# First modulation in column groups, tokens ahead of weights, and gate products one step later: a hybrid diffusion block on one core

## The chip, the cores and the metric

The kernel runs on one core of a Trainium2 chip. The metric is device time in microseconds (us), as the median of several executions. One more execution was taken with the hardware profiler; everything said of single instructions comes from it.

## What is computed

One layer of a diffusion backbone with 256 latent and 256 context tokens of width 2048, in float32.

- Two modulation vectors, one for the latent stream and one for the context: `silu(c) @ w_mod + b_mod`, 12288 wide. Its first 4096 columns are the shift and the scale of the first norm, and both streams need them; the others are needed for the latent stream alone.
- `h = rmsnorm(x) * (1 + scale) + shift` for both streams, then one projection `h @ w_in` to 7168 columns: q, two forget gates, v and an output gate for eight heads (HGRN2), and the input and the gate of a second recurrence (RG-LRU).
- HGRN2: a gated linear recurrence in both directions per head. RG-LRU: a depthwise convolution, then per block of 128 channels two gates `sigmoid(xc @ wa + ba)` and `sigmoid(xc @ wx + bx)` per direction, and a linear scan in both directions.
- The output projection, a gated residual, a second norm and modulation, a GEGLU MLP with a width-3 convolution (5632 wide), and the last gated residual.

## The kernel before, in words

All large products run in a split form: a float32 weight block is turned into a rounded high half (ACT, line 165) and the low half (DVE, line 180), tokens likewise, and three products (high-high, high-low, low-high) are added. A plain float32 product needs no split, and shows in the profile as two records.

The work is a list of **entries**, one per weight block of up to 1 MB. `run` (line 213) goes through them in order: for each chunk of an entry it emits the halves that are due (`split_to`, two halves ahead), then one step of every live generator (`step`, line 191), then the entry's products. So what a generator emits at one step stands on PE ahead of that chunk's products. A weight block lands in a ring of three buffers (`fetch`, line 140, on SP's queue); a buffer is asked for again only when its block has been used, or split where it has halves.

**First stage** (lines 287 to 411, 497 to 628). Entries 0 to 31 are the first modulation, 8 groups of 512 columns in 4 blocks each, shift and scale in turn (`add_mod1`, line 307). A block holds 4 x 128 rows of the weights by 512 columns. In blocks 0 to 15 (`whole`) the stationary operand is the 128 x 2 pair of both streams' vectors, in float32 (line 317). In blocks 16 to 31 weights are split and the stationary operand has 4 columns, high and low halves of both vectors (lines 323 and 324); the 4 x 2 table `sel` adds them up. When a group is whole, `mod1_sums` (line 335) copies it to SBUF and turns it into columns with four small products (line 343), and `mod1_scale` (line 354) makes the modulated tokens for four chunks of 128 channels: the high half on ACT (line 370), the value again on DVE or POOL (line 372), the low half on DVE (line 374). Between them stand 12 early entries (`add_early`, line 383): four groups of channels, three entries each, for the first six 128-column blocks of the projection, 24 products in each entry. Their place is the list `due` (line 404). The first entry of the list has to see every modulated chunk emitted before it (`after=("h1_gen",)`).

Tokens come in four quarters of 1 MB (`load_x`, line 500). The first is asked for after three weight blocks; the others from `first_norm` (line 596), one a step. `first_norm` squares them (ACT, line 603), adds them up (DVE, lines 605 to 609), gets sums over channels by products (`token_sums`), the inverse root, a broadcast over partitions (`spread`), and multiplies the tokens on POOL (line 623).

**Mixer stage** (lines 668 to 998). The other 50 blocks of the projection run in the order of `ORDER`. Three long chains go on beside them, a step per chunk: `mod2_all`, which accumulates the second modulation on DVE (line 689); the tree over a head's tokens (`tree`, line 866); and `rg_all`, one `rg_chain` (line 753) for each of the eight blocks of the second recurrence. A chain makes the convolved tokens, their high half `xh` (line 767) and low half `xl` (line 768) on DVE, yields, and emits the gates' six products of direction 0 (`gates(0)`, lines 776 to 778). At the end of a head the square of its output is written over `qa` (line 955), summed by two products (line 960), and copied by DVE in the same step (line 961). `qa` has one buffer, and so the next head's first write (line 872) waits for those products. `g_gen` (line 973) broadcasts a head's norm into one of the two small banks that the gates use too, and reads it on DVE (line 980).

```
    for c in range(e["nt"]):
        split_to(ahead(i, c))
        ...
        step()
        e["mm"](c, (lambda h: ring[e["half0"] + h]) if e["nh"] else fetched[i])
```

Of the kernel before, what the change touches and what calls it, by code (L numbers as in the profile page):

```python
# [17 lines left out]
KC = D // 128  # L18
T = 256
# [30 lines left out]
def dit_block_kernel(  # L50
# [55 lines left out]
    def P(name, k=0, n=1):  # L106
        o = _SM[name] + k
        return sm[:, o:o + n]

    ident = cp.tile([128, 128], F32, name="ident")  # L110
    masks = cp.tile([128, 7, 128], U8, name="masks")
    sel = cp.tile([4, 2], F32, name="sel")
    ones = cp.tile([128, 1], F32, name="ones")
    dve.memset(ones, 1.0)

# [132 lines left out]
    def tasks_after(gen):  # L248
        gens.insert(sum(g.__name__ not in BACK for g in gens), gen)
# [57 lines left out]
    def add_mod1(g, q, after, whole):  # L307

        rows = 2 if whole else 4

        def mm(c, get):
            if q == 0:
                mod1["ps"] = sbank(g // 4)
            ps = mod1["ps"][0:rows, :]
            for k in range(4):
                if whole:
                    pe.matmul(ps, cs[:, :, 4 * q + k], get[:, k * 512:(k + 1) * 512],  # L317
                              start=(q == 0 and k == 0), stop=(q == 3 and k == 3))
                    continue
                wh, wl = get(k // 2)  # L320
                cc = c4[:, 4 * q + k, :]
                s = slice(k % 2 * 512, (k % 2 + 1) * 512)
                pe.matmul(ps, cc, wh[:, s], start=(q == 0 and k == 0), stop=False)  # L323
                pe.matmul(ps, cc, wl[:, s], start=False, stop=(q == 3 and k == 3))  # L324

        def done():
            if q == 3:
                tasks_after(after(mod1["ps"], sel if rows == 4 else ident[0:2, 0:2]))
        add_entry(src=wmod[g, q], nt=1, nh=0 if whole else 2, mm=mm, done=done)


    s1 = cp.tile([128, 2, KC], F32, name="s1")
    sh1 = cp.tile([128, 2, KC], F32, name="sh1")

    def mod1_sums(ps, sel):
        n = sel.shape[0]
        sb = tp.tile([4, 512], F32, name="msb", tag="msb", bufs=2)[0:n, :]
        act.activation(sb, ps[0:n, :], AF.Copy)
        yield
        if n == 4:  # L340
            yield
        for j in range(4):
            pe.matmul(ps[:, 2 * j:2 * j + 2], sb[:, j * 128:(j + 1) * 128], sel, start=True, stop=True)
        yield
        return ps[:, 0:8].rearrange("p (j w) -> p w j", w=2)

    def mod1_shift(g):
        def gen(ps, sel):
            v = yield from mod1_sums(ps, sel)
            b = P("bm", 4 * g, 4)[:, None, :].to_broadcast([128, 2, 4])  # L350
            dve.tensor_tensor(sh1[:, :, 4 * g:4 * g + 4], v, b, op=OP.add)
        return gen

    def mod1_scale(g):
        def h1_gen(ps, sel):
            v = yield from mod1_sums(ps, sel)
            b = P("bm", 16 + 4 * g, 4)[:, None, :].to_broadcast([128, 2, 4])
            g0 = P("g", 4 * g, 4)[:, None, :].to_broadcast([128, 2, 4])
            d = s1[:, :, 4 * g:4 * g + 4]
            dve.tensor_tensor(d, v, b, op=OP.add)  # L360
            dve.scalar_tensor_tensor(d, d, 1.0, g0, op0=OP.add, op1=OP.mult)
            if g:
                yield
            while not xdone:
                yield
            for kc in range(4 * g, 4 * g + 4):
                f = tp.tile([128, 512], F32, name="hf", tag="hf", bufs=2)
                for w in range(2):
                    t = slice(w * 256, (w + 1) * 256)
                    act.activation(h1["hh"][:, kc, t], xk(kc)[:, t], AF.Identity,  # L370
                                   bias=sh1[:, w, kc:kc + 1], scale=s1[:, w, kc:kc + 1])
                    (pool if 0 < g < 3 else dve).tensor_scalar(
                        f[:, t], xk(kc)[:, t], s1[:, w, kc:kc + 1], sh1[:, w, kc:kc + 1], op0=OP.mult, op1=OP.add)
                dve.tensor_tensor(h1["hl"][:, kc, :], f, h1["hh"][:, kc, :].bitcast(F32), op=OP.subtract)
                if kc % 2:
                    yield
        return h1_gen


# [21 lines left out]
        add_entry(src=wearly[g, third], nt=2, nh=1, mm=mm, done=done, after=("h1_gen",))  # L401


    due = iter((15, 17, 19, 23, 25, 27, 29, 31, 32, 32, 32, 32))
    todo = [(g, third) for g in range(4) for third in range(3)]
    n = next(due)
    for i in range(32):
        g, q = divmod(i, 4)
        g, kind = divmod(g, 2)
        add_mod1(4 * kind + g, q, (mod1_shift, mod1_scale)[kind](g), i < 16)  # L410
        while todo and n == i + 1:
            add_early(*todo.pop(0))
            n = next(due, None)
# [80 lines left out]
            add_down(half, u)  # L494


    nc.sync.dma_start(sel, sel_d)
    fetch()

    def load_x(q):  # L500
        nc.sync.dma_start(xk(4 * q, 4), xs[:, 4 * q:4 * q + 4, :])
    load_x(0)
    nc.sync.dma_start(ident, ident_d)
    mf32 = tp.tile([128, 7 * 128], F32, name="mf32")


    cs = cp.tile([128, 2, KC], F32, name="cs")
    c4 = cp.tile([128, KC, 4], F32R, name="c4")
# [3 lines left out]
    cv = cs.rearrange("p w k -> p k w")  # L512
    c4v = c4.rearrange("p k (w s) -> p k w s", s=2)
    act.activation(c4v[:, :, :, 0], cv, AF.Copy)
    dve.tensor_tensor(c4v[:, :, :, 1], cv, c4v[:, :, :, 0].bitcast(F32), op=OP.subtract)

    lb = cp.tile([128, 2 * NH], F32, name="lb")
    oml = cp.tile([128, 2 * NH], F32, name="oml")
# [42 lines left out]
    def sqrt_table():  # L561

        act.activation(dummy, ones, AF.Sqrt)
# [30 lines left out]
    xdone = []  # L594

    def first_norm():
        qs = tp.tile([128, 2, 512], F32, name="qs0")
        for q in range(4):
            if q < 3:
                load_x(q + 1)  # L600
            for i in range(4 * q, 4 * q + 4, 2):
                sq = tp.tile([128, 2, 512], F32, name="sq", tag="sq", bufs=2)
                act.activation(sq, xk(i, 2), AF.Square)
                if i:
                    dve.tensor_tensor(qs, qs, sq, op=OP.add)
                else:
                    dve.tensor_copy(qs, sq)
# [145 lines left out]
    def rg_chain(b, x):  # L753
# [17 lines left out]
        def gates(d):  # L771
            pg = {}
            for w in (1, 0):
                pg[w] = sbank()
                c = slice((2 * d + w) * 128, (2 * d + w + 1) * 128)
                pe.matmul(pg[w], wh[:, c], xh, start=True, stop=False)
                pe.matmul(pg[w], wh[:, c], xl, start=False, stop=False)
                pe.matmul(pg[w], wl[:, c], xh, start=False, stop=True)
            return pg
        pg = gates(0)  # L780
        yield
        for d in range(2):
            k = 8 * d + b
            r, iv, th, t = (hq.tile([128, 512], F32, name=n, tag=n) for n in ("r", "iv", "th", "t"))
            for w, dst, bn in ((1, iv, "bx"), (0, r, "ba")):
                act.activation(dst, pg[w], AF.Sigmoid, bias=P(bn, k))
            yield
            act.activation(th, r, AF.Tanh, scale=sp4[:, k:k + 1])
# [77 lines left out]
    def tree(h, q):  # L866
# [477 lines left out]
```

## Time and profile before

| what | value |
|---|---|
| median of 3 executions | 1631.26 us (1630.3 to 1632.11) |
| the profiled execution | 1630.65 us |
| its span, from the first to the last instruction | 1628.9 us |
| PE, TensorE's products | busy 1566.8 us, 96% |
| DVE | busy 1207.4 us, 74% |
| ACT | busy 891.8 us, 55% |
| POOL | busy 121.0 us, 7% |
| DMA | 329.66 MB, 202 GB/s over the span |
| mean granted clock of TensorE | 0.984 of 2.4 GHz |

The span is the stretch that the profile covers; the execution's own time is 1.75 us more. PE is TensorE's products, PEld its weight loads, which lie beside products. A share of busy time is an average over stages with different limits, so a stage is read by itself. In a timeline, a bracket gives the idle time of the engine before an instruction and what ended it. A product's record is longer than its share of the engine, since products overlap in the array: the distance from start to start is its price.

### The profile page before, as it was taken

To read this page: it belongs to the slowest core of one execution; us is meant where nothing else is said; L and a number is where in the kernel's file an instruction comes from. 1 tells how busy PE (TensorE), PEld (TensorE's weight loads), DVE (VectorE), ACT (ScalarE), POOL (GpSimd) and SP (SyncE) were. 2 spreads that over 40 slices of the span, in tenths; PEclk is the share of its full clock that TensorE was granted. 3 is DMA by queue.
4 is the path that set the end of the run, shared out by engine and by line. 5 is a ranking of instruction groups with operands and counts; after the bars stand their busy time and mean duration, and the time that the engine had idled before them with its cause. 6 is when DMAs were issued, how large, how long until landed. Compare 5 with 4: busy or idle time off the path is not lost.

```text
span 1628.9 us, 25405 instructions
## 1 busy us (share of the span) xinstructions
PE 1566.8 (96%) x9904; PEld 1371.2 (84%) x9904; DVE 1207.4 (74%) x2033; ACT 891.8 (55%) x1284; POOL 121.0 (7%) x101
## 2 busy tenths in 40 slices
PE   7999899999999999899999999999999999999997
PEld 1355687778788888799999999999999999888886
DVE  2666597889888769678658788888888877656656
ACT  2355685767674456486455644444444445455553
POOL 0511000000000000000220111111111111000000
PEclk9999999999999999999999999999999999999999
DMA  8676544455455565536862466666666555655552
GB/s 355 236 283 225 193 162 149 158 172 174 167 197 199 183 206 186 183 124 238 318 224 94 171 228 230 226 231 226 229 227 227 201 181 190 221 184 197 191 200 110
DMA packets 75584, 329.66 MB, mean 202 GB/s; under 512 B 8392, under 2 KB 8520, under 8 KB 45128
## 3 DMA queue, kind: packets, MB, share of 16 engines
q1 hardware_dynamic: 75176, 327.53, 56.9%
q8 instruction: 77, 1.26, 0.3%
q10 hardware_dynamic: 288, 0.52, 0.1%
q14 instruction: 43, 0.35, 0.1%
HBM read 325.92 MB, written 2.10 MB: 201 GB/s over the span
## 4 chain that ended last, share of the span: by engine, by line
PE 79%; DVE 11%; ACT 4%; issue 3%; DMA 2%; POOL 1%; SPq 0%; DVEq 0%; ACTq 0%; POOLq 0%
PE mb L266 12%; PE mb L267 12%; PE mb L268 12%; PE mb L458 5%; PE lv L266 5%; PE lv L267 5%; PE lv L268 5%; PE lv L458 4%; PE sd L458 4%; PE sd L317 3%; DVE wl L180 2%; PE xb L458 2%; DVE macc L689 2%; PE sd L324 1%; PE sd L323 1%
## 5 line engine op out<-in xcount | busy, mean ns | idle before, releaser
L165 ACT ACTIVATE wh<-wf 128x1024 fp32r<-128x1024 f32 x424 | 445.3, 1058 | 508.4 <-PE mb L267 166.5
L180 DVE TENSOR_TENSOR wl<-wf,wh 128x1024 fp32r<-128x1024 f32 x440 | 535.7, 1223 | 155.1 <-ACT wh L165 151.2
L266 PE MATMUL mb<-hh,wh 128*128 128x512 f32 (+1 forms) x800 | 282.9, 354 | 0.0
L268 PE MATMUL mb<-hh,wl 128*128 128x512 f32 (+1 forms) x800 | 273.4, 342 | 0.0
L267 PE MATMUL mb<-hl,wh 128*128 128x512 f32 (+1 forms) x800 | 273.2, 342 | 0.0
L266 PE MATMUL mb<-h2h,wh 128*128 128x258 f32 x672 | 190.6, 284 | 0.0
L268 PE MATMUL mb<-h2h,wl 128*128 128x258 f32 x672 | 190.2, 283 | 0.0
L267 PE MATMUL mb<-h2l,wh 128*128 128x258 f32 x672 | 190.1, 283 | 0.0
L266 PE MATMUL lv<-h2h,wh 128*128 128x258 f32 x656 | 186.0, 284 | 0.0
L268 PE MATMUL lv<-h2h,wl 128*128 128x258 f32 x656 | 185.6, 283 | 0.0
L267 PE MATMUL lv<-h2l,wh 128*128 128x258 f32 x656 | 185.5, 283 | 0.0
L268 PEld LDWEIGHTS mb<-hh,wl 128*128 128x128 f32 x800 | 152.8, 191 | 17.9
L267 PEld LDWEIGHTS mb<-hl,wh 128*128 128x128 f32 x800 | 153.7, 192 | 15.9
L266 PEld LDWEIGHTS mb<-hh,wh 128*128 128x128 f32 x800 | 153.5, 192 | 15.3
L689 DVE SCALAR_TENSOR_TENSOR macc<-wm,cs,macc 128x512 f32<-128x512 f32 x180 | 136.3, 757 | 7.3 <-DMA wm<-in_wmod_dram 6.2
L267 PEld LDWEIGHTS mb<-h2l,wh 128*128 128x128 f32 x672 | 127.4, 190 | 0.0
L268 PEld LDWEIGHTS mb<-h2h,wl 128*128 128x128 f32 x672 | 126.9, 189 | 0.0
L266 PEld LDWEIGHTS mb<-h2h,wh 128*128 128x128 f32 x672 | 126.8, 189 | 0.0
L267 PEld LDWEIGHTS lv<-h2l,wh 128*128 128x128 f32 x656 | 124.4, 190 | 0.0
L268 PEld LDWEIGHTS lv<-h2h,wl 128*128 128x128 f32 x656 | 123.9, 189 | 0.0
L266 PEld LDWEIGHTS lv<-h2h,wh 128*128 128x128 f32 x656 | 123.7, 189 | 0.0
L1040 DVE TENSOR_TENSOR al<-actt,ah 128x256 fp32r<-128x256 f32 x88 | 37.8, 431 | 86.2 <-ACT ah L1039 86.2
(344 smaller groups left out, 2861.8 us busy)
## 6 DMA issues: line engine op xcount, KB each, us to landing
wf<-in_wup_dram SPq DMA_DIRECT2D x88, 1024.0 KB, 4.9
wm<-in_wmod_dram SPq DMA_DIRECT2D x256, 256.0 KB, 5.1
wf<-in_win_dram SPq DMA_DIRECT2D x50, 1024.0 KB, 4.8
wf<-in_wdn_dram SPq DMA_DIRECT2D x44, 1024.0 KB, 4.8
wf<-in_wmod_dram SPq DMA_DIRECT2D x32, 1024.0 KB, 5.7
wf<-in_wout_dram SPq DMA_DIRECT2D x16, 1024.0 KB, 5.1
wf<-in_wearly_dram SPq DMA_DIRECT2D x12, 512.0 KB, 5.5
oy<-in_xs_dram SPq DMA_DIRECT2D x2, 1024.0 KB, 13.4
```

The source lines that it names most:

```text
L165: act.activation(wh, w, AF.Copy)
L180: lo.tensor_tensor(wl, fetched[j][:, h * H:(h + 1) * H], wh.bitcast(F32), op=OP.subtract)
L266: pe.matmul(ps, wh[:, w], hh, start=(i == 0), stop=False)
L267: pe.matmul(ps, wh[:, w], hl, start=False, stop=False)
L268: pe.matmul(ps, wl[:, w], hh, start=False, stop=(i == KC - 1))
L317: pe.matmul(ps, cs[:, :, 4 * q + k], get[:, k * 512:(k + 1) * 512], start=(q == 0 and k == 0), stop=(q == 3 and k == 3))
L323: pe.matmul(ps, cc, wh[:, s], start=(q == 0 and k == 0), stop=False)
L324: pe.matmul(ps, cc, wl[:, s], start=False, stop=(q == 3 and k == 3))
L458: pe.matmul(dn["ps" + str(half)][tb * 2 + n], a[:, t], w[:, s], start=(kc == 0 and first), stop=(kc == NJ - 1 and last))
L689: dve.scalar_tensor_tensor(acc, w, cc, acc, op0=OP.mult, op1=OP.add)
L1040: dve.tensor_tensor(al, actt[:, kc, :], ah.bitcast(F32), op=OP.subtract)
```

## The change

It has four parts. (1) All 32 blocks of the first modulation take float32 products, none is split. The stationary operand is padded to 32 columns (`cpad`), and the four products of a block go to four groups of 32 columns of TensorE and to four groups of 32 partitions of one bank; the table `sel4` adds the four groups up in the small products that turn sums into columns. (2) All tokens are loaded ahead of the first weight block, the norm's sums are made in one step, and the multiplication of the tokens goes from POOL to DVE; the modulated value is made on ACT, and DVE makes its high and low halves. (3) The list `due` puts early entries further forward. (4) In `rg_chain` a yield stands ahead of `gates(0)`, and the one in the loop moves behind the tanh; a head's square goes to a buffer of the tag `qc`, and the copy of its sums comes a step later.

```diff
-    sel = cp.tile([4, 2], F32, name="sel")
...
+    cpad = tp.tile([128, KC, 32], F32, name="cpad")
+    sel4 = tp.tile([128, 2], F32, name="sel4")
+
+    def add_mod1(g, q, after):
         def mm(c, get):
             if q == 0:
                 mod1["ps"] = sbank(g // 4)
-            ps = mod1["ps"][0:rows, :]
             for k in range(4):
-                if whole:
-                    pe.matmul(ps, cs[:, :, 4 * q + k], get[:, k * 512:(k + 1) * 512],
-                              start=(q == 0 and k == 0), stop=(q == 3 and k == 3))
-                    continue
-                wh, wl = get(k // 2)
-                cc = c4[:, 4 * q + k, :]
-                s = slice(k % 2 * 512, (k % 2 + 1) * 512)
-                pe.matmul(ps, cc, wh[:, s], start=(q == 0 and k == 0), stop=False)
-                pe.matmul(ps, cc, wl[:, s], start=False, stop=(q == 3 and k == 3))
+                pe.matmul(mod1["ps"][32 * k:32 * k + 32, :], cpad[:, 4 * q + k, :], get[:, k * 512:(k + 1) * 512],
+                          start=(q == 0), stop=(q == 3), tile_position=(0, 32 * k))
...
+    def mod1_sums(ps):
+        sb = tp.tile([128, 512], F32, name="msb", tag="msb", bufs=2)
+        act.activation(sb, ps, AF.Copy)
         yield
-        if n == 4:
-            yield
         for j in range(4):
-            pe.matmul(ps[:, 2 * j:2 * j + 2], sb[:, j * 128:(j + 1) * 128], sel, start=True, stop=True)
-        yield
+            pe.matmul(ps[:, 2 * j:2 * j + 2], sb[:, j * 128:(j + 1) * 128], sel4, start=True, stop=True)
...
-            if g:
-                yield
             while not xdone:
                 yield
             for kc in range(4 * g, 4 * g + 4):
                 f = tp.tile([128, 512], F32, name="hf", tag="hf", bufs=2)
                 for w in range(2):
                     t = slice(w * 256, (w + 1) * 256)
-                    act.activation(h1["hh"][:, kc, t], xk(kc)[:, t], AF.Identity,
-                                   bias=sh1[:, w, kc:kc + 1], scale=s1[:, w, kc:kc + 1])
-                    (pool if 0 < g < 3 else dve).tensor_scalar(
-                        f[:, t], xk(kc)[:, t], s1[:, w, kc:kc + 1], sh1[:, w, kc:kc + 1], op0=OP.mult, op1=OP.add)
+                    act.activation(f[:, t], xk(kc)[:, t], AF.Identity, bias=sh1[:, w, kc:kc + 1], scale=s1[:, w, kc:kc + 1])
+                dve.tensor_copy(h1["hh"][:, kc, :], f)
                 dve.tensor_tensor(h1["hl"][:, kc, :], f, h1["hh"][:, kc, :].bitcast(F32), op=OP.subtract)
-                if kc % 2:
-                    yield
...
-    due = iter((15, 17, 19, 23, 25, 27, 29, 31, 32, 32, 32, 32))
+    due = iter((11, 13, 15, 19, 21, 23, 27, 29, 32, 32, 32, 32))
...
-    nc.sync.dma_start(sel, sel_d)
-    fetch()
-
     def load_x(q):
         nc.sync.dma_start(xk(4 * q, 4), xs[:, 4 * q:4 * q + 4, :])
-    load_x(0)
+    for q in range(4):
+        load_x(q)
     nc.sync.dma_start(ident, ident_d)
+    fetch()
...
+    dve.memset(cpad, 0.0)
+    dve.tensor_copy(cpad[:, :, 0:2], cs.rearrange("p w k -> p k w"))
+    dve.tensor_tensor(sel4, ident[:, 0:2], ident[:, 32:34], op=OP.add)
+    for j in (64, 96):
+        dve.tensor_tensor(sel4, sel4, ident[:, j:j + 2], op=OP.add)
...
     def first_norm():
+        sqrt_table()
         qs = tp.tile([128, 2, 512], F32, name="qs0")
-        for q in range(4):
-            if q < 3:
-                load_x(q + 1)
-            for i in range(4 * q, 4 * q + 4, 2):
...
-            yield
+        for i in range(0, KC, 2):
...
         sums = token_sums([qs[:, 0, :]], 4, lbank)
-        yield
         c = rq[:, :, 0:4]
         rsqrt(c[:, 0, :], sums, 1.0 / D, c[:, 1, :], c[:, 2, :])
         yield
         pb = spread(c[:, 0, :], 4, lbank)
-        yield
         rb0 = tp.tile([128, 512], F32, name="rb0")
         act.activation(rb0, pb, AF.Copy)
         for kc in range(KC):
-            pool.tensor_tensor(xk(kc), xk(kc), rb0, op=OP.mult)
+            dve.tensor_tensor(xk(kc), xk(kc), rb0, op=OP.mult)
...
+        yield
         pg = gates(0)
         yield
         for d in range(2):
...
                 act.activation(dst, pg[w], AF.Sigmoid, bias=P(bn, k))
-            yield
             act.activation(th, r, AF.Tanh, scale=sp4[:, k:k + 1])
+            yield
             act.activation(r, r, AF.Exp, scale=sp8[:, k:k + 1])
...
-        sq = qa[:, 0, :]
+        sq = hq.tile([128, T], F32, name="qc", tag="qc", bufs=3)
         act.activation(sq, po, AF.Square)
         yield
         pq = lbank()
         for b in range(2):
             pe.matmul(pq[:, b:b + 1], sq[:, b * 128:(b + 1) * 128], ones, start=True, stop=True)
+        yield
         dve.tensor_copy(ssq[:, 2 * h:2 * h + 2], pq[:, 0:2])
```

## Rows read from the trace of the kernel before

**Rows 1.** Stretches: from:to and length, busy us (instructions) by engine, PEclk, DMA, GB/s

```profile
core 0: us, PE busy (x) PEld busy (x) DVE busy (x) ACT busy (x) POOL busy (x), PEclk, DMA share, GB/s
...
0.00:8.64 8.64, 0.00 (x0) 0.03 (x1) 0.45 (x3) 1.75 (x3) 0.19 (x4) 1.00 0.80 294
8.64:20.00 11.36, 11.36 (x21) 2.00 (x22) 2.05 (x3) 3.22 (x4) 0.00 (x0) 1.00 1.01 405
...
70.00:163.00 93.00, 87.04 (x365) 51.34 (x363) 58.69 (x72) 50.81 (x61) 12.34 (x17) 0.96 0.68 249
...
189.00:760.00 571.00, 543.26 (x3173) 477.51 (x3172) 468.76 (x816) 374.05 (x563) 0.00 (x0) 0.97 0.52 175
```

**Rows 2.** Chain of waits, first 200 us: start us, us, what

```profile
49.35 13.82 PE sd L317 x32
...
187.89 0.25 PE xb L394
```

**Rows 3.** Timeline of PE, split blocks: start us, us, instruction

```profile
102.28 0.40 PE L323 MATMUL sd<-wh,c 128*4 128x512 f32 x1
...
106.92 0.40 PE L323 MATMUL sd<-wh,c 128*4 128x512 f32 x1
```

**Rows 4.** Timeline of PE, from block 31 to the end of the early projections

```profile
161.78 0.39 PE L324 MATMUL sd<-wl,c 128*4 128x512 f32 x1
162.84 1.05 PE L343 MATMUL sd<-sel,msb 4*128 4x2 f32 x8 [0.68 <-ACT msb L338]
...
171.82 0.50 PE L394 MATMUL mb<-hh,wl 128*128 128x512 f32 x1 [1.57 <-DVE wl L180]
...
173.53 0.39 PE L392 MATMUL mb<-hh,wh 128*128 128x512 f32 x1
...
187.27 0.39 PE L392 MATMUL xb<-hh,wh 128*128 128x512 f32 x1
```

**Rows 5.** Groups by line, DVE, 0 to 50 us: busy us, mean ns, idle before

```profile
L605 DVE TENSOR_TENSOR qs<-qs,sq 128x1024 f32<-128x1024 f32 x7 | 8.6, 1225 | 5.9 <-ACT sq L603 5.6
...
L607 DVE COPY qs<-sq 128x1024 f32<-128x1024 f32 x1 | 0.7, 694 | 12.6 <-ACT sq L603 12.6
```

**Rows 6.** DMA issues: KB each, median us from issue to landing

```profile
wf<-in_wup_dram SPq DMA_DIRECT2D x88, 1024.0 KB, 4.9
```

**Rows 7.** Waits of PE, from 188 us on: us in total, times, longest

```profile
PE sd L776 <- DVE xh L767: 16.7, 6, 4.5
PE sd L776 <- DVE oy L980: 4.1, 1, 4.1
...
PE sd L777 <- DVE xl L768: 0.7, 4, 0.2
```

**Rows 8.** Timeline of PE, the two longest waits of the gates' products

```profile
199.58 0.76 PE L776 MATMUL sd<-xh,gh 128*128 128x512 f32 x1 [4.46 <-DVE xh L767]
...
447.93 0.76 PE L776 MATMUL sd<-xh,gh 128*128 128x512 f32 x1 [3.95 <-DVE xh L767]
```

**Rows 9.** Stretches (columns as in rows 1) behind waits of the gates' products

```profile
199.00:205.00 6.00, 5.42 (x13) 4.06 (x14) 5.96 (x10) 4.83 (x8) 0.00 (x0) 0.52 0.79 286
...
351.00:355.00 4.00, 4.00 (x12) 3.16 (x11) 3.97 (x8) 2.19 (x4) 0.00 (x0) 0.57 0.25 66
447.50:454.00 6.50, 6.07 (x14) 4.56 (x15) 6.40 (x14) 0.72 (x2) 0.00 (x0) 0.50 0.81 295
682.00:697.00 15.00, 8.16 (x37) 6.52 (x36) 11.80 (x24) 7.72 (x14) 0.00 (x0) 0.66 0.39 132
```

**Rows 10.** A stretch of the mixer stage (columns as in rows 1)

```profile
360.00:380.00 20.00, 20.00 (x114) 17.34 (x113) 19.67 (x40) 15.34 (x27) 0.00 (x0) 1.00 0.49 172
```

**Rows 11.** Line 960 of a head's end, who waited for it: us, times

```profile
  DVE ssq L961: 16.5, 4
  DVE qa L872: 11.2, 3
```

**Rows 12.** Timeline of DVE, end of the second recurrence's block 7

```profile
740.36 0.42 DVE L810 TENSOR_TENSOR oy<-oy,r 128x256 f32<-128x256 f32 x1
...
747.00 0.42 DVE L818 TENSOR_TENSOR oy<-oy,gl 128x256 f32<-128x256 f32 x1 [1.20 <-ACT gl L816]
```

More of the change, by code (lines that the diff above doesn't have):

```diff
@@ L305, in dit_block_kernel @@
     mod1 = {}
-    def add_mod1(g, q, after, whole):
-        rows = 2 if whole else 4
+    cpad = tp.tile([128, KC, 32], F32, name="cpad")
+    sel4 = tp.tile([128, 2], F32, name="sel4")
+    def add_mod1(g, q, after):
         def mm(c, get):
@@ L313, in mm, with gen @@
                 mod1["ps"] = sbank(g // 4)
-            ps = mod1["ps"][0:rows, :]
             for k in range(4):
-                if whole:
-                    pe.matmul(ps, cs[:, :, 4 * q + k], get[:, k * 512:(k + 1) * 512],
-                              start=(q == 0 and k == 0), stop=(q == 3 and k == 3))
-                    continue
-                wh, wl = get(k // 2)
-                cc = c4[:, 4 * q + k, :]
-                s = slice(k % 2 * 512, (k % 2 + 1) * 512)
-                pe.matmul(ps, cc, wh[:, s], start=(q == 0 and k == 0), stop=False)
-                pe.matmul(ps, cc, wl[:, s], start=False, stop=(q == 3 and k == 3))
+                pe.matmul(mod1["ps"][32 * k:32 * k + 32, :], cpad[:, 4 * q + k, :], get[:, k * 512:(k + 1) * 512],
+                          start=(q == 0), stop=(q == 3), tile_position=(0, 32 * k))
         def done():
             if q == 3:
-                tasks_after(after(mod1["ps"], sel if rows == 4 else ident[0:2, 0:2]))
-        add_entry(src=wmod[g, q], nt=1, nh=0 if whole else 2, mm=mm, done=done)
+                tasks_after(after(mod1["ps"]))
+        add_entry(src=wmod[g, q], nt=1, nh=0, mm=mm, done=done)
     s1 = cp.tile([128, 2, KC], F32, name="s1")
     sh1 = cp.tile([128, 2, KC], F32, name="sh1")
[L335 to L338, printed above, removed]
+    def mod1_sums(ps):
+        sb = tp.tile([128, 512], F32, name="msb", tag="msb", bufs=2)
+        act.activation(sb, ps, AF.Copy)
         yield
-        if n == 4:
-            yield
         for j in range(4):
-            pe.matmul(ps[:, 2 * j:2 * j + 2], sb[:, j * 128:(j + 1) * 128], sel, start=True, stop=True)
-        yield
+            pe.matmul(ps[:, 2 * j:2 * j + 2], sb[:, j * 128:(j + 1) * 128], sel4, start=True, stop=True)
         return ps[:, 0:8].rearrange("p (j w) -> p w j", w=2)
     def mod1_shift(g):
-        def gen(ps, sel):
-            v = yield from mod1_sums(ps, sel)
+        def gen(ps):
+            v = yield from mod1_sums(ps)
             b = P("bm", 4 * g, 4)[:, None, :].to_broadcast([128, 2, 4])
@@ L354, in mod1_scale, with h1_gen @@
     def mod1_scale(g):
-        def h1_gen(ps, sel):
-            v = yield from mod1_sums(ps, sel)
+        def h1_gen(ps):
+            v = yield from mod1_sums(ps)
             b = P("bm", 16 + 4 * g, 4)[:, None, :].to_broadcast([128, 2, 4])
@@ L409, in dit_block_kernel @@
         g, kind = divmod(g, 2)
-        add_mod1(4 * kind + g, q, (mod1_shift, mod1_scale)[kind](g), i < 16)
+        add_mod1(4 * kind + g, q, (mod1_shift, mod1_scale)[kind](g))
         while todo and n == i + 1:
@@ L494, in dit_block_kernel @@
             add_down(half, u)
-    nc.sync.dma_start(sel, sel_d)
-    fetch()
     def load_x(q):
         nc.sync.dma_start(xk(4 * q, 4), xs[:, 4 * q:4 * q + 4, :])
-    load_x(0)
+    for q in range(4):
+        load_x(q)
     nc.sync.dma_start(ident, ident_d)
+    fetch()
     mf32 = tp.tile([128, 7 * 128], F32, name="mf32")
     cs = cp.tile([128, 2, KC], F32, name="cs")
-    c4 = cp.tile([128, KC, 4], F32R, name="c4")
     sg = tp.tile([128, 32], F32, name="csg")
@@ L511, in dit_block_kernel @@
     dve.tensor_tensor(cs.rearrange("p w k -> p (w k)"), sg, P("c", 0, 32), op=OP.mult)
[L512 to L515, printed above, removed]
+    dve.memset(cpad, 0.0)
[3 more added lines that the diff above has]
+        dve.tensor_tensor(sel4, sel4, ident[:, j:j + 2], op=OP.add)
     lb = cp.tile([128, 2 * NH], F32, name="lb")
@@ L596, in first_norm @@
     def first_norm():
+        sqrt_table()
         qs = tp.tile([128, 2, 512], F32, name="qs0")
-        for q in range(4):
-            if q < 3:
-                load_x(q + 1)
-            for i in range(4 * q, 4 * q + 4, 2):
[L602 to L607, printed above, removed]
-            yield
+        for i in range(0, KC, 2):
+            sq = tp.tile([128, 2, 512], F32, name="sq", tag="sq", bufs=2)
+            act.activation(sq, xk(i, 2), AF.Square)
+            if i:
+                dve.tensor_tensor(qs, qs, sq, op=OP.add)
+            else:
+                dve.tensor_copy(qs, sq)
         dve.tensor_tensor(qs[:, 0, :], qs[:, 0, :], qs[:, 1, :], op=OP.add)
@@ L786, in rg_chain @@
                 act.activation(dst, pg[w], AF.Sigmoid, bias=P(bn, k))
+            act.activation(th, r, AF.Tanh, scale=sp4[:, k:k + 1])
             yield
-            act.activation(th, r, AF.Tanh, scale=sp4[:, k:k + 1])
             act.activation(r, r, AF.Exp, scale=sp8[:, k:k + 1])
```

## The prediction

> **What bounds the kernel now.** I began with the table of stretches [rows 1]. TensorE is busy 95% of 189 to 760 us and 94% of 70 to 163, so it is the bound; the DMA engines run full (405 GB/s) only in the first 20 us, and PE does nothing before 8.64. So in the first stage I count the order of PE's products, and further on PE's idle time.
>
> The chain of waits then gives the price of a product of the first modulation [rows 2]: 32 records in 13.82 us, 0.432 each. A float32 product leaves two records, so one weight block (four products, 1 MB) costs 3.46. In the split form [rows 3] twenty records lie 4.64 us apart, 0.232 each; eight to a block make 1.86. An early projection is 24 products at 0.229 (60 steps in 13.74 us [rows 4]), 5.5 us. Block 31's last record ends at 161.78 + 0.39 = 162.2 [rows 4] and the last early product at 188.1 [rows 2]: a tail of 26 us. In that tail PE waits once, 1.57, for the low half of a weight that stands on DVE behind the last modulated tokens.
>
> In the mixer stage PE's waits [rows 7] name one cause above all: the gates' first product waits for xh, six times, 16.7 us, plus 0.7 for xl and once 4.1 for a bank that DVE's line 980 still reads. The two longest are in [rows 8]. Behind long ones the granted clock is low [rows 9]: 0.50 of 2.4 GHz, the lower of its two levels, behind the wait that ended at 447.93.
>
> **The change, part by part: the first stage.** Removed are the split of 16 blocks (32 conversions on ACT, 32 subtractions on DVE) and its products; all 32 blocks now take four float32 products, each on 32 columns of its own. What such products cost beside one another is nowhere in the trace. Ends: all eight records one after another, 3.46 a block, plus the time in flight that a record has after its successor's start (0.39 against a step of 0.229 [rows 4], 0.16) at four changes of column group, makes 4.1; all four groups at once, 0.86 and a little, 0.95. I take a value between, 1.9, from the order of the program: the two records of one product use the same columns and follow each other, so only the second of one product and the first of the next can run together; that is four slots of 0.432 a block, 1.73, and one half-covered slot where a run of blocks ends.
>
> Tokens first: the small parameters (0.34 MB), 4.19 MB of tokens, ident and a block make 5.65 MB ahead of the first product. By 8.64 us 294 GB/s had brought 2.54 MB; the rest at 405 takes 7.7 [rows 1]: block 0 lands at 16.3 instead of 8.6. The sum of squares now stands on DVE behind the addition that waits for ident (about 14 us), and its own additions are 8.6 + 0.7 us [rows 5] and a last one of 0.6: about 25. The token sums are placed ahead of block 2, so PE, free at 20.8, waits there to about 25.5; the sums (1.05, as the like products of [rows 4]), block 2, the norm's small steps and the broadcast (2.4, an estimate) and block 3 end near 32.7. The ring holds three blocks, so block 5 was asked for only after block 2 (28.4) and lands 4.9 later [rows 6]; from there a block comes every 2.55 us (1.05 MB at 411 GB/s, an estimate close to the 405), and block 10 ends near 49.7. The sixteen multiplications by the norm move from POOL to DVE, 0.62 each (half of 1.23 [rows 5]), 10 us, from 29 to 40: the first modulated tokens are due at 44, so they hide; without that cover they would push the first early projection one for one.
>
> From there PE has 21 blocks at 1.9 (39.9), eight early projections at 5.5 (44.0) and five sums of 1.05 (5.3): 89. Each early projection also waits for its halves, since the ring gives its buffer back only after the subtraction: about 1 us each, 8. Block 31 ends at 147. In the tail DVE makes two passes a chunk instead of three; I take 0.7 off: 25.3, so 172 against 188.1. **Minus 16 us**; 0.95 a block would give minus 32, 4.1 plus 39.
>
> A rule of the Trainium skill speaks against it: TensorEngine Tiling (Array Packing), Key Properties, says that changing the tiling mode drains TensorE. No row shows such a change; as an estimate, some 32 changes between 32 and 128 columns at the 0.16 in flight would make the sum 1599 instead of 1594.
>
> **The gates.** With a further step between xl and the gates' products PE has one more chunk of twelve products (2.74 us) to do before them. Of the six waits only two are longer: 4.46 leaves 1.7 and 3.95 leaves 1.2 [rows 8]; the other 8.3 and the 0.7 go. The 4.1 for the bank [rows 7] leaves 1.4 at most, as the broadcast then belongs to an earlier step. Removed: 5.5 + 9.0 + 2.7 = 17.2. Clock: (1 - clock) times the stretch, idle time left out, is 2.9, 1.7, 3.2 and 3.0 in the four of [rows 9], about 10 in all. Together 27. I give 7 back: DVE is nearly full where this happens (19.67 of 20 us [rows 10]), and PE's idle time is when it catches up, so some of it returns as waits for weights' low halves. Tanh one yield earlier changes no work.
>
> The head's square goes into a free buffer, and its sums' copy one step later: DVE now waits 16.5 and 11.2 us for these products [rows 11]. DVE is not the bound, so I count nothing for it but the 20 kept above. The gates' chain gets a step longer: block 7's ends at 740.4 and its gated product comes at 747.0 [rows 12], 6.6 of slack for 2.74. **Minus 20 us**, between minus 28 (all kept) and plus 3 (all comes back, and one step more at the end).
>
> **Sum.** The profiled execution took 1630.65 (span 1628.9 and 1.75 around it), 0.6 under the median shown: 1630.65 - 16 - 20 = 1594.6, say 1594. A measurement here tells about 0.2%, 3.3 us, from no change.
>
> **Rivals.**
> A. All four column groups at once, 0.95 a block. For: in the sum above the groups share no columns. Against: the second record of a product stands in program order ahead of the next group's first. DMA then sets the pace (what comes after block 10 is 21 blocks and eight halves of one, 25 times 2.55 or 64 us, and the ring's late returns, about 2 us at each early projection, make it 82): block 31 at 130.4, stage end 155.7, minus 32 - 20: 1578. The Trainium skill gives up to 4x for 32 columns in TensorEngine Tiling (Array Packing), Theoretical Speedup, and 2.38x for three column tiles in TensorE: Matmul & The Clock Gate, Part 3; no row here shows either.
> B. The groups take turns. Place: every block of the first modulation; price: 3.43 to 4.1 instead of the old mean of 2.66. It costs time in this stage from 2.6 a block on (the same working then ends at 188.2), and the kernel is slower as a whole from 3.45 on, where the stage's plus 20 has eaten the gates. At 4.1 block 31 ends at 202 and the stage at 227: plus 39 - 20, 1650. For: the trace has no two records of one engine side by side beyond the time in flight. Against: nothing in the program makes one group wait for another; they write different partitions.
> C. The gates' wait only moves: DVE is full, xh is later by as much as PE is earlier, and weights' low halves come late instead. For: [rows 10]. Against: over 189 to 760 DVE is busy 82% [rows 1], and it loses the waits of [rows 11]. Then minus 16 alone: 1614.
>
> **How the numbers follow.** Forecast (1583 to 1606 by the bounds of its two terms, 10 to 20 and 14 to 28) 0.47; A 0.22; B 0.20, of which 0.11 is slower, 0.06 within 0.2% (no time in flight: 1631) and 0.03 faster; C 0.11. Faster 0.83, same 0.06, slower 0.11. The range takes in the forecast, A from 1568 and C, and the lowest part of B: 1568 to 1630, leaving out 0.18.
>
> **What would show it.** Start to start of the new products: 0.43 between records with two on the way at once (a block in 1.7 to 1.9) is the forecast; 0.2 is A; 0.43 with eight in a row is B. First product near 16.3, a gap ahead of block 2 near 4 us, last early product near 172. In the mixer stage no wait for xh over 2 us, and windows behind them at full clock; if waits for low halves add up to more than 10 us, C is right. The prediction is wrong if the stage ends after 180, or if the time from there to the end falls by less than 10 us.

## The result, and the profile after

The changed kernel takes 1604.24 us (median of 4 runs, 1603.96 to 1605.46) against 1631.68 (1630.3 to 1634.98) for the kernel before on the same chip: 0.983 of it, with a 95% interval of 0.9813 to 0.9847. That is 27.4 us less, where 36 (16 + 20) were forecast; the direction was right, and the time lies in the range. The top of the page after:

```profile
span 1602.3 us, 25254 instructions
## 1 busy us (share of the span) xinstructions
PE 1528.5 (95%) x9904; PEld 1363.0 (85%) x9904; DVE 1167.8 (73%) x2021; ACT 864.4 (54%) x1253; POOL 89.7 (6%) x69
...
PEclk8788999999999999999999999999999999999999
```

Its mean granted clock is 0.977, where before had 0.984. The first four digits of the last line, the first 160 us, are now below 9. The timeline of PE marks the two ends by which I split the gain: the last early product, and the first product of the output projection (the row with `mh`). The last row is that of the kernel before.

```profile
176.68 0.40 PE L376 MATMUL xb<-hh,wl 128*128 128x512 f32 x1
...
732.02 0.39 PE L267 MATMUL mb<-mh,wl 128*128 128x256 f32 x1 [0.64 <-DVE wl L179]
...
760.00 0.39 PE L268 MATMUL mb<-mh,wl 128*128 128x256 f32 x1 [0.87 <-DVE wl L180]
```

The first stage ends at 177.1 instead of 188.1 [rows 2]: 11.0 us. From there to the output projection it is 554.9 us; before, that first product stood at 760.00, 571.9 after the stage's end: 17.0 us. The remaining 870 us are 1.4 longer. Forecast were 16 and 20, so the stage gave 5 too little and the gates 3.

**The first stage.** The start in the timeline of PE:

```profile
16.56 1.93 PE L315 MATMUL sd<-wf,cpad 128*32 128x512 f32 x8 [16.56 <-DVE qs L584]
18.96 1.53 PE L315 MATMUL sd<-wf,cpad 128*32 128x512 f32 x8 [0.47 <-DMA wf<-in_wmod_dram]
25.76 1.87 PE L562 MATMUL lv<-ones,qs 128*128 128x1 f32 x8 [5.26 <-DVE qs L587]
...
38.37 1.07 PE L315 MATMUL sd<-wf,cpad 128*32 128x512 f32 x8 [1.98 <-DMA wf<-in_wmod_dram]
...
50.87 1.94 PE L315 MATMUL sd<-wf,cpad 128*32 128x512 f32 x8 [1.84 <-DMA wf<-in_wmod_dram]
53.22 0.80 PE L374 MATMUL mb<-hh,wh 128*128 128x512 f32 x1 [0.42 <-ACT wh L164]
...
55.88 0.63 PE L374 MATMUL mb<-hh,wh 128*128 128x512 f32 x1
56.31 0.63 PE L375 MATMUL mb<-hl,wh 128*128 128x512 f32 x1
...
63.18 1.92 PE L315 MATMUL sd<-wf,cpad 128*32 128x512 f32 x16
65.04 1.05 PE L332 MATMUL sd<-sel,msb 128*128 128x2 f32 x8
```

Sixteen records, two blocks, take 1.92 us: 0.96 a block (0.95 by the chain of waits, which gives such pairs 1.90 and 1.85), where 3.46 stood before [rows 2]. The single block at 50.87 takes twice what the one at 38.37 takes, and the early products at 55.88 stand 0.43 apart where [rows 4] have 0.229. The stretches say why (columns as in rows 1; the last row is that of the kernel before):

```profile
40.00:62.00 22.00, 17.40 (x60) 8.41 (x61) 13.44 (x46) 7.06 (x12) 0.00 (x0) 0.53 0.76 288
...
16.50:53.00 36.50, 24.63 (x120) 8.69 (x120) 26.72 (x59) 15.30 (x23) 1.32 (x1) 0.69 0.84 330
53.00:100.00 47.00, 40.93 (x192) 24.92 (x192) 12.25 (x26) 10.31 (x16) 0.00 (x0) 0.84 0.65 248
100.00:152.00 52.00, 42.38 (x217) 25.80 (x214) 9.68 (x16) 9.95 (x15) 0.00 (x0) 0.88 0.75 281
152.00:177.00 25.00, 25.00 (x100) 19.94 (x100) 10.49 (x15) 12.63 (x21) 0.53 (x1) 0.91 0.55 205
...
60.00:160.00 100.00, 85.37 (x420) 53.02 (x420) 24.71 (x42) 26.06 (x41) 0.53 (x1) 0.88 0.67 252
...
60.00:160.00 100.00, 94.71 (x384) 53.24 (x383) 68.13 (x90) 51.64 (x62) 18.70 (x23) 0.97 0.67 244
```

From 60 to 160 us PE is busy for 85 us instead of 95 and DVE for 25 instead of 68: the work that the change removes is gone. But the granted clock of these 100 us is 0.88, where before it was 0.97. It is a mix of the two levels: between waits PE runs at 1.2 GHz for some microseconds, and then the early products, which the change does not touch, take nearly twice their time. (The first block takes 1.93 as well, though the profile gives 1.00 for the stretch from 16.5 to 18.5 us; why, stays open.) The chain of waits names loads of `in_wearly`, the early entries' weights, and one of `ident`:

```profile
3.06 10.90 DMA ident<-in_ident_dram
...
65.59 7.22 DMA wf<-in_wearly_dram
...
100.67 8.57 DMA wf<-in_wearly_dram
```

**The mixer stage.** Waits of PE from 178 us on (us in total, times, longest):

```profile
PE sd L752 <- DVE oy L958: 4.2, 1, 4.2
PE sd L570 <- ACT iv L763: 2.1, 1, 2.1
PE sd L752 <- DVE xh L743: 1.8, 2, 1.4
...
PE mb L267 <- DVE wl L179: 1.0, 2, 0.6
PE sd L753 <- DVE xl L744: 0.8, 4, 0.2
```

The wait for xh has gone from 16.7 [rows 7] to 1.8. The one for a bank that g_gen still reads (line 958 now, 980 before) stays at 4.2 [rows 7], and a wait of 2.1 for the gates' sigmoid is new. Behind these two, from 664 to 676 us, the granted clock is 0.81.

### The profile page after: what moved, and what is told of

Same layout as the page of the kernel before. It is cut to its first block, busy times and chain, and to the rows that moved or that the text cites. A ratio compares the mean times of both kernels' runs of the same rounds, so it can differ in the third digit from the quotient of the medians.

```text
span 1602.3 us, 25254 instructions
## 1 busy us (share of the span) xinstructions
PE 1528.5 (95%) x9904; PEld 1363.0 (85%) x9904; DVE 1167.8 (73%) x2021; ACT 864.4 (54%) x1253; POOL 89.7 (6%) x69
## 4 chain that ended last, share of the span: by engine, by line
PE 81%; DVE 10%; ACT 4%; DMA 2%; issue 2%; SPq 0%; DVEq 0%; ACTq 0%
PE mb L265 13%; PE mb L266 13%; PE mb L267 13%; PE mb L440 5%; PE lv L265 5%; PE lv L267 5%; PE lv L266 5%; PE lv L440 4%; PE sd L440 4%; PE xb L440 2%; DVE wl L179 2%; DMA wf<-in_wearly_dram 1%; DVE macc L665 1%; PE sd L315 1%; PE lv L928 1%
## 5 line engine op out<-in xcount | busy, mean ns | idle before, releaser
L164 ACT ACTIVATE wh<-wf 128x1024 fp32r<-128x1024 f32 x392 | 413.6, 1059 | 527.1 <-PE mb L266 185.0
L179 DVE TENSOR_TENSOR wl<-wf,wh 128x1024 fp32r<-128x1024 f32 x408 | 498.9, 1225 | 189.6 <-ACT wh L164 187.9
```

What stands on the lines that cost most here:

```text
L164: act.activation(wh, w, AF.Copy)
L179: lo.tensor_tensor(wl, fetched[j][:, h * H:(h + 1) * H], wh.bitcast(F32), op=OP.subtract)
```

## The experiments

Two theories stood against each other after this. **Loads**: the early weights come late, since one ring of three buffers and one queue serve them and the modulation's blocks. **Clock**: the short products leave waits, the granted clock falls in them, and what follows runs at half speed. The forecast's own, **price** (a block costs 1.9), had to fall or stand as well. Times are medians; the ratio is to the kernel before on the same chip.

**1 and 2. The two halves of the change alone.** The first is the kernel before with the change's edits of the mixer, the second the changed kernel without them.

```diff
+        yield
         pg = gates(0)
...
-            yield
             act.activation(th, r, AF.Tanh, scale=sp4[:, k:k + 1])
+            yield
...
-        sq = qa[:, 0, :]
+        sq = hq.tile([128, T], F32, name="qc", tag="qc", bufs=3)
...
+        yield
         dve.tensor_copy(ssq[:, 2 * h:2 * h + 2], pq[:, 0:2])
```

> The kernel before with the mixer stage's edits alone (yield ahead of the gates' products, tanh ahead of the yield, head's square in a qc buffer and its copy a step later). If the two halves of the change are independent, the mixer's part is what the two traces show between the end of the early projections and the first wait of the output projection: 571.9 us before, 554.9 after, so minus 17 us and some 1 us lost later: 1615 us. If part of that came from where the shorter first stage leaves DVE and the DMA queues, less: 1620 or more. Waits of PE for xh fall from 16.7 us to under 4.

Measured: 1614.85, 0.9909 [0.9893, 0.9926], so 16.2 us less, as expected. PE's wait for xh is 1.1.

> The changed kernel with the mixer stage's edits undone: the first stage's part alone. The traces give 188.1 against 177.1 us at the last early product, so minus 11 and 1620 us if the parts add. PE's waits for xh come back to 14 to 20 us. If the parts help each other, it is over 1623.

Measured: 1623.34, 0.9951 [0.9934, 0.9967], 7.7 us less (both stand against the same 1631.06). PE's wait for xh is back:

```profile
PE sd L752 <- DVE xh L743: 15.2, 6, 4.1
```

The halves add up to 23.9 of the 27.4: neither needs the other. 1623.34 lies just over the 1623 that was to mean that they help each other; but each of the three numbers is known to some 3 us, so the 3.5 left over may be nothing. In this profile the first stage, whose program is the changed kernel's, ends at 174.2, 3 us before the changed kernel's own. So much can lie between two executions, and a single profile's stage end is read to about 3 us.

**3 and 4. The number of column groups.** All four products of a block in one group, and in two. The diff is that of two; with one, o is 0 and the first and last product of all four start and stop the sum. Left out of it: the copy and the small sums take only the rows that are in use.

```diff
-    pe.matmul(mod1["ps"][32 * k:32 * k + 32, :], cpad[:, 4 * q + k, :], get[:, k * 512:(k + 1) * 512],
-              start=(q == 0), stop=(q == 3), tile_position=(0, 32 * k))
+    o = 32 * (k % 2)
+    pe.matmul(mod1["ps"][o:o + 32, :], cpad[:, 4 * q + k, :], get[:, k * 512:(k + 1) * 512],
+              start=(q == 0 and k < 2), stop=(q == 3 and k > 1), tile_position=(0, o))
...
```

> The changed kernel with all four products of a block on the same 32 columns, added up in the same 32 partitions (the copy and the small sums then take two rows, as in the kernel before). A block should cost 8 records of 0.43, 3.4 us, instead of 0.95. Theory that PE's products of the first modulation still set the stage: 32 times 2.5, plus 79 us, stage end 256. Theory that waits for the early weights' halves and the half clock set it: those hide part of it; PE's own work becomes the bound at 32 x 3.45 + 66 + 10 and 16 us before the first block, stage end 200 to 212, plus 23 to 35 us, 1627 to 1640.

Measured: 1644.14 in one run. Two blocks and the stretch from 60 to 160 us:

```profile
67.77 7.05 PE L315 MATMUL sd<-wf,cpad 128*32 128x512 f32 x16
...
60.00:160.00 100.00, 99.40 (x321) 46.15 (x319) 19.47 (x39) 17.15 (x27) 0.00 (x0) 1.00 0.59 214
```

> The changed kernel with two groups of 32 columns: products 0 and 2 on one, 1 and 3 on the other. If groups run beside each other whole, a block costs 4 records in a row, 1.75 us, plus 0.8 us on each of 32 blocks. Theory that the products' price sets the stage: plus 26 us, stage end 203, 1630. Theory that the stage waits for the early weights' halves and for the clock: most of it falls into waits, and PE stays busier, so that the clock falls less; stage end 174 to 182, 1600 to 1609.

Measured: 1609.9, 0.9878 [0.9858, 0.9897]. The same rows:

```profile
61.90 3.63 PE L316 MATMUL sd<-wf,cpad 128*32 128x512 f32 x16
...
60.00:160.00 100.00, 92.12 (x411) 50.82 (x410) 21.68 (x37) 23.18 (x37) 0.00 (x0) 0.98 0.70 255
```

A block costs 3.5, 1.8 and 0.96 with one, two and four groups, the granted clock being 1.00 in all three rows: products in different groups run beside one another, almost whole. With one group PE is full, at full clock, and the stage ends at 212.9, not at the 256 of a stage that the products' price alone would set. From two groups to four 32 blocks lose 0.86 each, 27 us, and the stage ends at 180.1 instead of 177.1, 5.7 us in the time: below 1.8 a block, the products no longer set the end. And the clock goes from 0.98 to 0.88 with them.

**5. Loads.** The early weights get two buffers of their own, so a load of theirs no longer needs the return of one of the shared three.

```diff
...
+            if entries[j]["nh"] == 1:
+                fetched[j] = tp.tile([128, H], F32, name="we", tag="we", bufs=2)
+            else:
+                fetched[j] = wp.tile([128, D], F32, name="wf", tag="wf", bufs=RING)
...
```

> The changed kernel with a ring of two buffers of their own for the early projections' weights, beside the ring of three for the modulation's blocks (the SBUF copy of the modulation sums gets one buffer less to make room). Theory that the early weights are late because their request waits for a buffer of the shared ring: ACT's wait for them falls from 45.9 us to under 20, the stage ends at 160 to 168, the kernel at 1588 to 1596. Theory that the half clock sets the stage: ends at 172 or later, 1600 or more.

Measured: 1600.74, 0.9806 [0.9792, 0.9821]; the stage ends at 172.5. Waits up to 178 us, in the changed kernel and with the ring, and with the ring two stretches and the last early product:

```profile
ACT wh L164 <- DMA wf<-in_wearly_dram: 45.9, 6, 11.6
...
ACT wh L171 <- DMA we<-in_wearly_dram: 34.9, 7, 9.4
```

```profile
40.00:62.00 22.00, 16.62 (x58) 7.82 (x59) 13.65 (x46) 7.05 (x12) 0.00 (x0) 0.53 0.85 341
60.00:160.00 100.00, 90.87 (x442) 57.75 (x441) 27.80 (x45) 28.23 (x43) 0.53 (x1) 0.86 0.70 273
...
172.10 0.39 PE L383 MATMUL xb<-hh,wl 128*128 128x512 f32 x1
```

ACT's wait for these weights falls from 45.9 to 34.9, not to under 20, and the time by 3.5. The intervals of this and the changed kernel's ratio overlap, so that gain is likely, not certain. PE is busy for 5.5 us more of the 100, at a mean clock of 0.86: the ring is a part at most, not all.

**6 and 7. Clock, with too much of it.** Products with a stationary operand of zeros keep PE busy: one ahead of each block, three ahead of each of nine early entries. The second kernel does it with the ring of 5.

```diff
+            pe.matmul(mod1["ps"], zt, zmov, start=(q == 0), stop=False)
             for k in range(4):
...
+            for i in range(3 if pad else 0):
+                pe.matmul(early[b], zt, zmov, start=(g == 0 and i == 0), stop=False)
```

> The changed kernel with products of zeros that add nothing to the sums: one float32 product (0.86 us) ahead of every block of the first modulation and three ahead of each of the nine early projections of the first three groups, in PE's waits. Theory that the half clock costs the stage: the granted clock from 60 to 160 us rises from 0.88 to over 0.97, the early projections take 5.5 us each, and the stage ends 5 to 9 us earlier although PE does some 50 us more; 1595 to 1600. Theory that the halves' arrival alone sets it: no earlier, 1604 to 1612.

> Both edits. If late weights and the half clock are two losses side by side, the gains add: stage end 155 to 163, 1582 to 1592. If the own ring leaves no waits, the zero products are only extra work for PE, and this is slower than the own ring alone by up to 20 us.

Measured: 1624.39, 0.9955 [0.994, 0.997], and 1622.92, 0.9949 [0.9932, 0.9966]. Both miss: the clock is 1.00, but PE is now busy for 99.25 and 99.67 of the 100 us, and the stage ends near 194. The 59 products lie where PE had work, too, and there each is paid for in full. So neither theory is decided by them.

**9. Clock, in the waits only.** The ring of 5, and 23 zero products where PE waits: ahead of blocks 2 to 10, 16 to 18 and 24 to 26 (one each), behind block 31 (two) and ahead of three early entries (two each).

```diff
+    zeros = set(range(2, 11)) | {16, 17, 18, 24, 25, 26}
...
+            if i in zeros:
+                pe.matmul(mod1["ps"], zt, zmov, start=(q == 0), stop=False)
...
```

> The kernel with the early weights' own ring, and products of zeros only where PE waits there: one ahead of blocks 2 to 10, 16 to 18 and 24 to 26, two ahead of the first early projection of each of the first three groups, two behind block 31 (23 products of 0.86 us, 20 us). Theory that the low clock behind these waits costs some 14 us: the granted clock from 60 to 160 us is over 0.96 instead of 0.86, no early entry takes over 6 us, the stage ends at 160 to 167 instead of 172.5, 1589 to 1596. Theory that the clock is only a sign of waits for DMA: stage end 171 to 180, 1599 to 1608.

Measured: 1593.95, 0.9766 [0.975, 0.9781]; the stage ends at 165.7.

```profile
40.00:62.00 22.00, 18.43 (x86) 7.60 (x83) 14.86 (x49) 7.05 (x12) 0.00 (x0) 1.00 0.94 375
60.00:160.00 100.00, 98.50 (x495) 60.01 (x494) 29.68 (x46) 31.83 (x49) 0.53 (x1) 1.00 0.72 280
...
165.35 0.39 PE L395 MATMUL xb<-hh,wl 128*128 128x512 f32 x1
```

From 40 to 62 us the clock is 1.00 where it is 0.53 in the changed kernel and with the ring alone; against the ring alone the stage ends 6.8 us sooner, and the whole too by the medians, whose ratios' intervals lie apart. (The profile is of the longest of its four runs, 1597.21.) Nothing but the zero products was added, and they only give PE more to do, so this is the clock.

**8 and 10. Inside the gates' step.** First, the changed kernel with the head's square and its sums as before; then, the broadcast that g_gen reads in another bank.

```diff
-        sq = hq.tile([128, T], F32, name="qc", tag="qc", bufs=3)
+        sq = qa[:, 0, :]
...
-        yield
         dve.tensor_copy(ssq[:, 2 * h:2 * h + 2], pq[:, 0:2])
```

> The changed kernel with the head's square back in qa and the copy of its sums in the same step; the gates' products stay one step later. Theory that the step between xl and the gates' products gives the mixer's gain and DVE's waits at a head's end are off the path: within 3 us of the changed kernel, 1602 to 1608. Theory that DVE's waits at a head's end (16.5 and 11.2 us before) made xh late: 1612 to 1620.

Measured: 1605.33, 0.9833 [0.9818, 0.9848], within 1.1 us of the whole. The square's own buffer is worth nothing that these runs can tell; the step between xl and the products is the gain (the tanh's earlier place is in this run too and was not taken by itself).

```diff
-        pb = spread(rso[:, 2 * h:2 * h + 2], 2)
+        pb = spread(rso[:, 2 * h:2 * h + 2], 2, xbank)
```

> The changed kernel with a head's broadcast in the bank of the second modulation's sums instead of one of the two that the gates use. PE's wait of 4.2 us for line 958 and the 2.1 us for the gates' sigmoid ahead of a broadcast go, and with them the low clock between 664 and 676 us: minus 4 to minus 9 us, 1595 to 1600. If another wait takes their place (the bank is shared with the sums of the second modulation, or xh comes just then): 1602 to 1606.

Measured: 1601.38, 0.9821 [0.9807, 0.9835], 2.9 us less by the medians and 1.5 by the ratios, whose intervals overlap: the gain is likely, not certain. The waits are plainer (PE, from 178 us on):

```profile
PE lv L879 <- DVE ad L868: 3.2, 2, 1.9
PE lv L918 <- DVE qa L913: 3.2, 2, 2.0
PE sd L752 <- DVE xh L743: 1.8, 2, 1.4
...
PE xb L570 <- DVE oy L958: 1.0, 1, 1.0
```

The 4.2 for the bank and the 2.1 for the sigmoid are gone, 6.3 in all; 1.0 comes back in the new bank, and the waits for `ad` and `qa`, two tiles of the tree over a head's tokens, grow by 1.8 and 2.2 (from 1.4 and 1.0): 1.3 us net. From 664 to 676 us the clock is 0.86, a little above the changed kernel's 0.81.

**11. All three together**: the ring, the zero products in the waits, the other bank.

> Own ring, zero products in the waits and the broadcast in the other bank together. The three act at different places, so if each does what is expected the gains add: 1583 to 1592. If the first two do nothing: 1595 to 1600.

Measured: 1591.07 (5 runs), 0.9752 [0.9739, 0.9765]. The stage ends at 164.7. By its median it is the fastest kernel here, 40 us under the kernel before and 13 under the changed one; its interval overlaps that of experiment 9, so what the other bank adds to it is not shown.

**12. The order of the loads.** The changed kernel with the first three weight blocks ahead of the tokens.

```diff
+    fetch()
     for q in range(4):
         load_x(q)
     nc.sync.dma_start(ident, ident_d)
-    fetch()
```

> The changed kernel with the first three weight blocks (3 MB) asked for ahead of the tokens instead of behind them. If the loads' order is hidden, that is if the stage is set by what comes behind block 10: first product near 9 us, blocks 0 to 2 done by about 17, the tokens 7.7 us later (3.15 MB at about 410 GB/s), block 10 still ends between 50 and 54, stage end within 2 us of 177, time within 2.5 us of the changed kernel's 1604.2. If the DMA stream in the first 50 us sets the stage: block 3 is asked for at about 10 instead of 18.5 us, the stream loses its holes (0.84 of 36.5 us busy, 5.8 us), block 10 ends near 48 and the stage 3 to 5 us earlier, time near 1600. If the norm is what the early projections wait for: the token sums come near 33 instead of 25.8, the multiplied tokens 7 us later, the first early projection near 58 instead of 53, time 2 to 5 us longer, near 1608.

Measured: 1612.62 (4 runs), 0.988 [0.9864, 0.9897], 8.4 us more than the changed kernel. Timeline of PE:

```profile
6.88 1.93 PE L315 MATMUL sd<-wf,cpad 128*32 128x512 f32 x8 [6.88 <-DMA wf<-in_wmod_dram]
9.28 1.56 PE L315 MATMUL sd<-wf,cpad 128*32 128x512 f32 x8 [0.46 <-DMA wf<-in_wmod_dram]
33.85 1.87 PE L562 MATMUL lv<-ones,qs 128*128 128x1 f32 x8 [23.01 <-DVE qs L587]
...
61.15 0.80 PE L374 MATMUL mb<-hh,wh 128*128 128x512 f32 x1 [0.39 <-ACT wh L164]
```

The first product comes 9.7 us sooner and does not matter; the token sums come 8.1 later (33.85 against 25.76), the first early product 7.9 later, the stage's end 6.6. PE's order has the token sums ahead of block 2, so it stands there for 23 us, all later blocks and the ring with it. So the norm of the tokens, not the first block, sets the start, and its delay goes through to the end: the third expectation names the cause and was too mild (near 1608), the other two are out. Of these two orders the change's is the better by 8.4 us. The chain of the changed kernel begins at the same place: the load of `ident`, behind the tokens, which ends at 13.96. The timeline of its DVE (idle time before, and what ended it, in the bracket):

```profile
13.98 0.16 DVE L494 TENSOR_TENSOR sel<-ident 128x2 f32<-128x2 f32 x1 [9.16 <-DMA ident<-in_ident_dram]
14.18 0.36 DVE L496 TENSOR_TENSOR sel<-sel,ident 128x2 f32<-128x2 f32 x2
14.45 0.69 DVE L586 COPY qs<-sq 128x1024 f32<-128x1024 f32 x1
15.24 9.74 DVE L584 TENSOR_TENSOR qs<-qs,sq 128x1024 f32<-128x1024 f32 x7
25.02 0.69 DVE L587 TENSOR_TENSOR qs<-qs 128x512 f32<-128x512 f32 x1
```

DVE stands idle for 9.16 us over a table of 64 KB, with squares ready behind it. To ask for `ident` ahead of the tokens would take that away; it was not tried, and what it is worth stays open. Nor were two parts of the change taken by themselves: the new list `due`, and the norm's multiplications on DVE instead of POOL.

## Why the prediction was partly right

**Right.** The first product came at 16.56 (16.3 forecast; the row names DVE, but block 0, asked for at 3.67, landed 12.7 later, at 16.4), the wait ahead of block 2 was 5.26 (4.7 in the working, "near 4" in the list of signs) and ended at 25.76 (25.5), and block 10 ended at 52.8 (49.7). DVE's multiplications by the norm end at 41.9, before the first modulated tokens are made at 48.8: hidden, as said, but for 0.65 us at 43.44, where PE waits for DVE's small steps that stand behind them. That the token sums carry every later step with them is borne out by experiment 12. The gates' extra step took the xh wait from 16.7 to 1.8, and no low-half waits took its place (1.0 against the 10 that would have meant C): rival C is out. The square and its copy are worth nothing that can be told, as counted. Three places of the working do not come out as told, none by more than 2 us: 14 + 8.6 + 0.7 + 0.6 is 23.9, not about 25; counted from block 5 at 33.3, block 10 would end at 48.0, and 49.7 follows from block 6; the four clock terms, idle time left out, are 2.6, 1.7, 3.0 and 2.8, still about 10.

**The step that failed: the price of a block and what it leads to.** I took 1.9 us, "from the order of the program", and put 0.95 with rival A. It is 0.96, and experiments 3 and 4 show where the argument was wrong: the second record of one product does not hold back the first of the next group. Two blocks went from 7.05 with one group to 1.92 with four, 3.7 times; the up to 4x of the Trainium skill's TensorEngine Tiling (Array Packing), Theoretical Speedup, agrees. Its rule in Key Properties, that a change of tiling drains TensorE, is not to be seen at 65.04 above, where 128 columns follow 32 columns 1.86 after the blocks' start, with no gap.

Yet the stage ended at 177, later than the 172 that the wrong price gave, and not at A's 155.7. The sum from block 10 on, corrected term by term: start 3.1 later; 21 blocks at 0.95 less, minus 20.0; PE idle 15.7 from 53 to 177 us (47 - 40.93 and 52 - 42.38), where "about 1 us each" made 8 and the tail had 1.6, so 6 more; and the clock, (1 - clock) times the busy time of the three stretches from 53 us on, 6.5 + 5.1 + 2.3 = 13.9. 172 + 3.1 - 20.0 + 6 + 13.9 makes 175; the other 2 us I cannot place, and the end varies by 3. So that the forecast's end came within 5 us is luck: a price 20 us too high in all stood against some 23 of waits and clock. Two terms were mis-sized, and one was not there: the sum of the stage had no term for the clock, though the one of the gates had, by the same rows [rows 9]. Of these terms the runs took away a part: experiment 5 likely 3.5 us by the loads, experiment 9 another 6.8 by the clock. Together they end the stage at 165.7, where the sum without both has 155.1; 14 of the zero products lie behind block 10 and by 0.86 each cost up to 12 us of that. The rest of the two terms is reckoned from rows, not shown by a run. Rival A's working lacked the clock too. Which part of the early loads' lateness is the ring's depth, and which the queue's order, the runs do not separate.

**The gates.** 20 forecast; 16.2 measured alone, 17.0 in the trace. The mis-sized term is the bank: the 4.1 was to leave 1.4 at most, "as the broadcast then belongs to an earlier step", but it stands at 4.2, and 2.1 for the sigmoid is new. In sum the waits for xh, xl, the bank and the sigmoid were 21.5 (16.7 + 0.7 + 4.1) and are 8.9 (1.8 + 0.8 + 4.2 + 2.1): 12.6 removed where the working had 17.2. PE's idle time in all falls from 28.4 us (188.14 to 760 us) to 15.2 (177.08 to 732.02), so 13.2; its busy time falls from 543.5 to 539.7 with as many records, 3173 and 3172. These 3.7 us stand against its 10 for the clock less 7 given back, and so the clock's net term came out near its size and the waits' 4 too large. That the 3.7 is the clock fits the same two stretches, 0.99 after against 0.97 before, but no run took it by itself. One sign was not met: behind the waits for the bank and the sigmoid the clock was 0.81, not full.

## What to carry to other kernels

Where a change makes the products of a stage shorter than its loads, count the clock next: products that the change does not touch run at half speed behind the new waits. Zero products paid here only where PE had nothing to do (23 in the waits took 6.8 us off, 59 spread over the stage put 22 on, experiments 9 and 7 against 5). And follow the chain that the stage's later work hangs on before pricing its first product: here the norm's sums set the start, and 8.1 us of delay in them became 8.4 in the whole.

## What the runs showed of the hardware that was not expected

- Float32 products of 32 columns in different column groups run beside one another with little lost: 3.5, 1.8 and 0.96 us for four products in one, two and four groups.
- The same products, run in less of PE's time and so with waits between them, ran at a lower granted clock: 1.00, 0.98 and 0.88 from 60 to 160 us with one, two and four groups, and 1.00 again with four groups, 23 zero products in the waits and the ring of experiment 5.
- A single block takes 1.07 us at 38.37, where the granted clock is 1.00 (38.3 to 39.5 us), and 1.94 at 50.87, where it is 0.50 (50.8 to 52.9): a price read from one short row can be off by a factor of two.
